# A decoder layer with 32 experts: pooling branch ahead of the state space scans on VectorE, bias-row product and second embedding projection later on TensorE

## The chip, the core and the metric

The kernel runs on one core of a Trainium2 chip. The metric is the device time of one execution in microseconds (us), median of several. The engines named below are PE (TensorE, matrix products), DVE (VectorE), ACT (ScalarE), POOL (GpSimd) and SP (SyncE, which here issues most of the transfers). Each engine works through its own instruction list; semaphores hold an instruction until what it reads is there.

## The reference

One layer over 512 tokens of width 1024, everything in float32. Cut to what the change touches:

```python
proj = h @ w_in                       # 512 x 3072: u_ssm | u_pool | gate_a | gate_b
y_ssm  = s5_branch(u_ssm, ...)        # linear recurrence over the 512 positions
y_pool = pool_branch(u_pool, ...)     # causal means over 2, 4, 8, 16 positions, minus u; group product; projection
merged = sigmoid(gate_a) * y_ssm + sigmoid(gate_b) * y_pool
h = layer_norm(alpha * h + merged @ w_out)
# mixture: top 4 of 32 experts per token, each expert g, u, down with biases
moe_out = sum_k weight_k * (((clip(u) + 1) * g * sigmoid(1.702 g)) @ w_down[e] + b_down[e])
ple = sigmoid(h @ w_ple_gate) * (p @ w_ple_proj)
h = layer_norm(alpha * h + moe_out + ple)
```

## The kernel before

Three stages follow one another. The **front** (to some 377 us) holds the dense work: the input projection, the scans, the pooling branch, the gates, `w_out`, the first layer norm, the routing and the embedding (`ple`) products. The **experts** follow, 32 of them in a fixed order, each with 12 weight tiles of 1 MB (four for gate, four for up, four for down) that SyncE loads into `eraw` tiles. A **tail** adds up and does the second layer norm.

*Products in the front.* A float32 product is made of three: both operands are split into a high and a low part (`split`, L103 to L104: ACT casts the high part, DVE subtracts for the low one), and `mm3` (L115 to L117) adds hi·hi, lo·hi and hi·lo in PSUM. A full product here is 128x128 times 128x512.

*The scans and the pooling.* `chan_major` generators make the projections channel by channel; a loop over 24 slots steps them and calls side work at fixed slots, from tables of four numbers each. `QVEC`, `QTAB`, `QMAT`, `QOUT`, `QST`, `QY` place the steps of the four scan groups: POOL makes tables of powers (`er`, `ei`), DVE makes `hre` and `him`, and `q_y` (L500 to L502) reads them on PE. `PVEC` = (4, 5, 7, 9) places `pool_vec` (L543), which for a window of 2 to 16 adds shifted copies on DVE (`wa`, L551 and L552), scales, and splits the result into `ph` (high part on ACT, low part on DVE); there is one buffer each of `wa` and `ph`. `PMAT` = (4, 6, 7, 9) places `pool_mat`, three products `tp<-ph` on PE, whose result is scaled, split and stored in `mh`, `ml`.

*Routing and the embedding.* `route_vec` picks the experts and ends with `ri` (L812), the list rows; POOL then scatters 16 times into the lists in memory, `lst` (L817). `route_cols` makes `ir`, the rows of the bias tables, takes it through a small product with `one` (L858) and casts it to `ib`. Behind the lists POOL loads them back: `ls` (L993) and, in four pieces, `ls4` (L996); DVE turns `ls4` into `ix4`, the scatter indices of the experts (a `ts` with `jc`, L182, shown in the trace as `ix<-ls,jc`). Overflow beyond the fixed list lengths is counted by a chain of small steps: `cps` and `pcc` (products L1027 and L1030), `bi`, `ov`, a product with `tri` (L1039) into `pps`, then `bx` and the count `nbx`. SyncE reads `nbx` into a register (L1448) ahead of the further `eraw` loads in its list.

The embedding is done in two halves of 512 columns. `ple_g`, and for the second half a loop at L1063 to L1080, make the gating products into `acc` tiles; `ple_p` (L934 to L936) projects `p`; `ple_mul` multiplies the two into `gl`. `base_b` (L945) adds the experts' down-biases to `h`, `base_out` adds `gl` and, for the second half, sends `h` to `acc_d` in memory. In the loop over four bundles of gating products, `base_b` comes with the middle two and `ple_p(1)` before the last.

*What sets the order.* Instructions are put on each engine's list by a scheduler that takes those that are ready by its own reckoning in the order of a priority, which is the order in the code; `tc.high_priority()` puts what it encloses first, `tc.issue_after(x)` puts what it encloses behind instruction x. On the chip each engine keeps the resulting list. Memory of the front that becomes free behind the last gating product is where most of the 16 `eraw` tiles lie: five are loaded at about 208 to 227 us, the others as front tiles are given up. The experts' first biases come through `bias_rows` (four gathers into `br`, by `ib`) and `bias_table` (`btab`).

Of the kernel before, what the change touches and what calls it, by code (L numbers as in the profile page):

```python
# [23 lines left out]
T, D, E, K = 512, 1024, 32, 4  # L24
# [17 lines left out]
EBUF = 2  # L42
ENG = 'SSSVP'
PVEC = (4, 5, 7, 9)
PMAT = (4, 6, 7, 9)
QVEC = (0, 4, 10, 15)
QTAB = (2, 4, 9, 14)
QMAT = (3, 8, 11, 17)
# [20 lines left out]
def _layer(top, tc, nc, x, xT, pT, ssm, ssm_d, log_step, w_in, w_val, w_glg, w_pg, pscale, w_pp,  # L69
           w_out, ln1_g, ln1_b, w_r, b_r, w_gate, b_gate, w_up, b_up, w_down, b_down, w_pleg,  # L70
           w_plep, ln2_g, ln2_b, out, dbg):
    V = nc.vector
# [14 lines left out]
    def tps():  # L87
        return psum.tile([128, 512], F32, tag="tp", name="tp", bufs=2)
# [489 lines left out]
    def at(slot, f, *a):  # L578
        side.setdefault(slot, []).append((f, a))

    for g in range(4):
        at(PVEC[g], lambda g: PV.update({g: pool_vec(g)}), g)
        at(PMAT[g], lambda g: pool_mat(g, PV[g]), g)
    for hs in range(4):
        for f_, sl in ((q_vec, QVEC), (q_tab, QTAB), (q_mat, QMAT), (q_out, QOUT), (q_state, QST), (q_y, QY)):
# [251 lines left out]
    def route_cols():  # L837
        col, cmp_ = RT["col"], RT["cmp"]
        tt(cmp_, col[:, None, :].to_broadcast([128, E, E]), ie[:, :, None].to_broadcast([128, E, E]), OP.is_equal)
        tt(cmp_, cmp_, ie[:, None, :].to_broadcast([128, E, E]), OP.mult)  # L840
        ef = mide.tile([128, 2, E], F32, name="ef")
        V.tensor_reduce(ef[:, 0], cmp_, axis=AX.X, op=OP.add)
        ts(eid, ef[0:1, 0], float(D), OP.mult)
        ts(ef[:, 1], ef[:, 0], float(NB), OP.mult)
        ir = mide.tile([1, E, NB, 2], BF16, name="ir")
        tt(ir, ef[0:1, 1][:, :, None, None].to_broadcast([1, E, NB, 2]), ie[0:1, None, :NB, None].to_broadcast([1, E, NB, 2]), OP.add)
        cf = mide.tile([128, 2, E], F32, name="cf")
        lo, hi = CAP.index(128), CAP.index(64)
        ts(cf[:, 0], col, float(hi), OP.is_lt, 32.0, OP.mult)
        ts(cf[:, 1], col, float(lo + CAP.count(128)), OP.is_lt, 32.0, OP.mult)  # L850
        tt(cf[:, 0], cf[:, 0], cf[:, 1], OP.add)
        ts(cf[:, 1], col, float(lo), OP.is_lt, -32.0, OP.mult)
        stt(cf[:, 0], cf[:, 0], 64.0, cf[:, 1], OP.add, OP.add)
        for i, v in enumerate((col, cf[:, 0])):
            V.tensor_copy(rowb[:, i], v[0:1, None, :].to_broadcast([1, NB, E]))
        pb = tps()
        for h_ in range(2):
            TE.matmul(pb[:, 2 * h_:2 * h_ + 2], lhsT=ir.rearrange("p e j a -> p (e j a)")[:, h_ * 128:(h_ + 1) * 128], rhs=one[0:1, 0:2], start=True, stop=True)  # L858
        V.tensor_copy(ib, pb[:, 0:4].rearrange("p (h a) -> p h a", a=2)[:, :, 0])
# [70 lines left out]
    def ple_p(n0, t_, o):  # L930
        wp = PW["p", n0]
        c_ = slice(t_ * 128, (t_ + 1) * 128)
        for kx in range(2):
            TE.matmul(o, lhsT=pth[:, kx, c_], rhs=wp[0][:, kx], start=kx == 0, stop=False)  # L934
            TE.matmul(o, lhsT=pth[:, kx, c_], rhs=wp[1][:, kx], start=False, stop=False)
            TE.matmul(o, lhsT=ptl[:, kx, c_], rhs=wp[0][:, kx], start=False, stop=kx == 1)  # L936
        PW["o", n0, t_] = o

    def ple_mul(n0, t_):
        tt(PW[n0, t_], PW["o", n0, t_], PW[n0, t_], OP.mult)  # L940
# [79 lines left out]
    with tc.issue_after(RT["ri"].ins):  # L1020
        for r_ in range(NB):
            V.tensor_copy(cn[:, :, r_], mk)
    NC_ = N_CAND
    cps = tps()[:NC_, :2]
    ones2 = one[:, 0:2]
    for t_ in range(4):
        TE.matmul(cps, lhsT=cn[:, t_].rearrange("p r e -> p (r e)"), rhs=ones2, start=t_ == 0, stop=t_ == 3)  # L1027
    pcc = tps()
    for i in range(2):
        TE.matmul(pcc[:NC_, 2 * i:2 * i + 2], lhsT=rowb[:, i].rearrange("p r e -> p (r e)"), rhs=one[0:1, 0:2], start=True, stop=True)  # L1030
    bi = mide.tile([128, 4], F32, name="bi")
    for r_ in range(NB):
        V.memset(bi[r_ * E:(r_ + 1) * E, 0:1], 128.0 * r_)
    tt(bi[:, 0:1], pcc[:NC_, 2:3], bi[:, 0:1], OP.add)
    stt(bi[:, 2:3], bi[:, 0:1], float(E), pcc[:NC_, 0:1], OP.mult, OP.add)
    ov = mide.tile([128, 2], BF16, name="ov")
    V.tensor_scalar(ov[:NC_], cps, bi[:NC_, 0:1], None, op0=OP.is_gt)
    pps = tps()
    TE.matmul(pps[:NC_, 0:2], lhsT=tri[:NC_, :NC_], rhs=ov[:NC_], start=True, stop=True)  # L1039
    TE.matmul(pps[:1, 256:258], lhsT=one[:NC_, 0:1], rhs=ov[:NC_], start=True, stop=True)  # L1040
    V.tensor_scalar(bi[:NC_, 1:2], ov[:NC_, 0:1], -1e6, 1e6, op0=OP.mult, op1=OP.add)
    tt(bi[:NC_, 1:2], pps[:NC_, 0:1], bi[:NC_, 1:2], OP.add)
    bx = late.tile([128, 4], I32, name="bx")
    nbx = late.tile([1, 1], I32, name="nbx")
    V.tensor_copy(bx[:NC_, 0:1], bi[:NC_, 1:2])
    V.tensor_copy(bx[:NC_, 2:3], bi[:NC_, 2:3])
    V.tensor_copy(nbx, pps[:1, 256:257])
    P.iota(bx[:NC_, 1:2], pattern=[[0, 1]], base=E, channel_multiplier=1)

    ple_wp(0)  # L1050
    for t_ in range(4):
        ple_p(0, t_, sacc())
        ple_mul(0, t_)
    with tc.issue_after(RT['ri'].ins):
        ple_w(1)
        ple_wp(1)
# [491 lines left out]
```

## Time and profile before

| what | us |
|---|---|
| median of 3 executions | 1495.27 |
| lowest and highest | 1493.91, 1495.96 |
| profiled execution, its device time | 1496.11 |
| its span in the trace | 1494.4 |
| PE busy in it | 1354.0 |
| DVE busy | 439.3 |
| ACT busy | 245.8 |
| POOL busy | 292.5 |

The profiled execution lies 0.84 us above the median, and 1.71 us of it lie outside the span. The mean granted clock of TensorE in it was 0.975. A row of a timeline reads: start in us, duration in us, engine, line of the kernel, operation, out<-in, shapes, count, and in brackets how long the engine was idle before it and what released it. Starts of neighbouring products lie closer than their durations, since products are pipelined. `tp`, `ss` and `acc` are PSUM tiles.

### The profile page before, as it was taken

Reading aid. Unit: us, or ns where it says so; the run is one execution under the profiler, and the core shown is the slowest. Engines: PE = TensorE matmul, PEld = TensorE weight load, DVE = VectorE, ACT = ScalarE, POOL = GpSimd, SP = SyncE. Lnnn points to the kernel's source line nnn. Section 1 sums busy time; section 2 is a strip of 40 time slices with the busy share of each in tenths; the row PEclk is TensorE's granted clock in tenths of the full one; section 3 lists DMA queues with packets and bytes.
Section 4 is the critical chain, followed back from the end, with each engine's and each line's share of the span. In section 5 each row is a group of like instructions: output and inputs, shape, how many; then the busy total and the mean of one; then the engine's idle time right before and its main releaser. Section 6 shows DMA issues by size and latency. Waiting matters only on the chain.

```text
span 1494.4 us, 41207 instructions
## 1 busy us (share of the span) xinstructions
PE 1354.0 (91%) x18454; PEld 874.6 (59%) x18454; DVE 439.3 (29%) x938; ACT 245.8 (16%) x435; POOL 292.5 (20%) x295
## 2 busy tenths in 40 slices
PE   8969999989799999998897989989889799799993
PEld 7858878767456666665454545545445455456651
DVE  7967657676211111111111101111111111011106
ACT  4534344151101010100000000110000000010011
POOL 0684110016202111111111111112111111110132
PEclk9989999999899999999999999999999999999996
DMA  7213244623999999999999999999999999999953
GB/s 249 85 44 89 59 159 155 217 99 137 351 403 393 397 387 383 396 396 385 386 393 391 391 398 389 397 393 389 387 388 393 383 392 397 378 390 403 404 184 134
DMA packets 105860, 468.58 MB, mean 314 GB/s; under 512 B 17837, under 2 KB 42865, under 8 KB 56528
## 3 DMA queue, kind: packets, MB, share of 16 engines
q1 hardware_dynamic: 88944, 446.12, 76.9%
q0 software_dynamic: 16736, 19.79, 6.1%
q8 instruction: 146, 2.39, 0.6%
q14 instruction: 34, 0.28, 0.1%
HBM read 453.23 MB, written 17.80 MB: 315 GB/s over the span
## 4 chain that ended last, share of the span: by engine, by line
DMA 51%; PE 35%; DVE 7%; POOL 4%; issue 2%; ACT 1%; SPq 0%; POOLq 0%; DVEq 0%; ACTq 0%
DMA eraw<-in_w_down_dram 17%; DMA eraw<-in_w_gate_dram 16%; DMA eraw<-in_w_up_dram 16%; PE acc L1124 13%; PE ss L1124 6%; PE acc L116 3%; PE acc L117 3%; PE acc L115 3%; POOL lst L817 1%; DMA br<-in_b_up_dram,ib 1%; PE acc L1131 1%; DVE h L190 1%; DVE lo L104 1%; PE acc L879 1%; PE tp L1140 1%
## 5 line engine op out<-in xcount | busy, mean ns | idle before, releaser
L1124 PE MATMUL acc<-eraw,xt 128*32 128x256 f32 x10880 | 615.5, 385 | 53.0 <-DMA eraw<-in_w_up_dram 50.0
L1124 PEld LDWEIGHTS acc<-eraw,xt 128*32 128x32 f32 x10880 | 349.1, 111 | 307.0 <-DMA eraw<-in_w_up_dram 68.7
L1124 PE MATMUL ss<-eraw,ht 128*32 128x256 f32 x5312 | 299.7, 380 | 23.0 <-DMA eraw<-in_w_down_dram 22.8
L1159 POOL DMA_INDIRECT acc_d<-y,ix x83 | 129.5, 1560 | 866.5 <-ACT y L1193 850.6
L1124 PEld LDWEIGHTS ss<-eraw,ht 128*32 128x32 f32 x5312 | 170.8, 110 | 148.0 <-DMA eraw<-in_w_down_dram 35.0
L1141 ACT COPY ht<-tp 128x512 f32<-128x512 f32 (+1 forms) x50 | 23.9, 516 | 650.9 <-PE tp L1140 650.9
L182 DVE TENSOR_SCALAR u<-acc 128x512 f32<-128x512 f32 (+1 forms) x51 | 30.6, 600 | 287.5 <-PE acc L1124 276.3
L180 DVE TENSOR_SCALAR g<-acc 128x512 f32<-128x512 f32 (+1 forms) x51 | 30.6, 602 | 275.1 <-PE acc L1124 274.9
L1005 DVE COPY xt<-tp 128x384 f32<-128x384 f32 (+2 forms) x32 | 16.4, 512 | 319.5 <-PE tp L1004 319.5
L1174 ACT ACTIVATE s<-g 128x512 f32<-128x512 f32 (+1 forms) x51 | 27.9, 559 | 270.7 <-DVE g L180 270.7
L104 DVE TENSOR_TENSOR lo<-raw,hi 128x1024 fp32r<-128x1024 f32 (+1 forms) x50 | 60.6, 1216 | 27.9 <-ACT hi L103 27.6
L103 ACT CAST hi<-raw 128x1024 fp32r<-128x1024 f32 (+1 forms) x53 | 54.9, 1036 | 75.4 <-PE acc L116 48.6
L115 PE MATMUL acc<-ahi,hi 128*128 128x512 f32 x160 | 63.9, 399 | 0.0
L117 PE MATMUL acc<-ahi,lo 128*128 128x512 f32 x160 | 63.7, 398 | 0.0
L116 PE MATMUL acc<-alo,hi 128*128 128x512 f32 x160 | 63.4, 396 | 0.0
L1011 POOL DMA_INDIRECT xg<-hd,ls x32 | 32.3, 1011 | 42.4 <-PE tp L1004 28.2
L1207 PE MATMUL acc<-btab,sel_e 128*128 128x512 f32 x102 | 28.3, 387 | 9.6 <-DVE btab L190 9.6
L117 PEld LDWEIGHTS acc<-ahi,lo 128*128 128x128 f32 x160 | 30.6, 191 | 6.6
L115 PEld LDWEIGHTS acc<-ahi,hi 128*128 128x128 f32 x160 | 30.8, 192 | 6.1
L116 PEld LDWEIGHTS acc<-alo,hi 128*128 128x128 f32 x160 | 30.6, 191 | 6.3
L1193 ACT ACTIVATE y<-ss,ls 128x256 f32<-128x256 f32 x83 | 33.8, 481 | 0.0
L186 DVE TENSOR_TENSOR g<-g,s 128x512 f32<-128x512 f32 (+1 forms) x51 | 29.2, 601 | 13.0 <-ACT s L1174 13.0
(404 smaller groups left out, 1303.8 us busy)
## 6 DMA issues: line engine op xcount, KB each, us to landing
eraw<-in_w_gate_dram SPq DMA_DIRECT2D x128, 1024.0 KB, 21.7
eraw<-in_w_up_dram SPq DMA_DIRECT2D x128, 1024.0 KB, 21.5
eraw<-in_w_down_dram SPq DMA_DIRECT2D x128, 1024.0 KB, 23.2
raw<-in_w_in_dram SPq DMA_DIRECT2D x23, 512.0 KB, 4.4
raw<-in_w_out_dram SPq DMA_DIRECT2D x8, 512.0 KB, 4.2
raw<-in_w_ple_gate_dram SPq DMA_DIRECT2D x8, 512.0 KB, 5.5
raw<-in_w_pool_proj_dram SPq DMA_DIRECT2D x4, 512.0 KB, 3.5
raw<-in_w_glu_val_dram SPq DMA_DIRECT2D x4, 512.0 KB, 3.5
```

What stands on the lines that cost most here:

```text
L103: S.copy(h, v)
L104: (lo_eng or V).tensor_tensor(l, v, h.bitcast(F32), op=OP.subtract)
L115: TE.matmul(o, lhsT=lh, rhs=rh, start=start, stop=False)
L116: TE.matmul(o, lhsT=lh, rhs=rl, start=False, stop=False)
L117: TE.matmul(o, lhsT=ll, rhs=rh, start=False, stop=stop)
L180: V.tensor_scalar(o, i, a, None, op0=op)
L182: V.tensor_scalar(o, i, a, b, op0=op, op1=op1)
L186: V.tensor_tensor(o, a, b, op=op)
L1011: P.indirect_dma_start(out=xg[:n_], out_offset=None, in_=hd, in_offset=bass.IndirectOffsetOnAxis(ap=lst_[:n_, 0:1], axis=0), bounds_check= ...
L1124: TE.matmul(os[b // 2][j * 32:(j + 1) * 32, b % 2 * 256:b % 2 * 256 + 256], lhsT=x_, rhs=w_[:, kk, j * 256:(j + 1) * 256], start=first and ...
L1159: q_ = P.indirect_dma_start(out=acc_d.rearrange("t (j c) -> (t j) c", j=4), out_offset=bass.IndirectOffsetOnAxis(ap=ix_[b], axis=0), in_=y ...
L1193: S.activation(y_[:, b * 256:(b + 1) * 256], py[b // 2][:, c_], AF.Copy, scale=w_.bitcast(F32))
```

## The change

Three things are done.

1. The four `pool_vec` calls run under high priority, and the third and fourth `pool_mat` are one slot later.
2. The product with `ir` and its cast become a function of their own, `route_ib`; it and the whole overflow chain are issued behind the first half's `ple_p`.
3. The second half's `ple_p` is issued behind the last gating product.

```diff
-PMAT = (4, 6, 7, 9)
+PMAT = (4, 6, 8, 10)
...
+    def pool_first(g):
+        with tc.high_priority():
+            PV[g] = pool_vec(g)
+
     for g in range(4):
-        at(PVEC[g], lambda g: PV.update({g: pool_vec(g)}), g)
+        at(PVEC[g], pool_first, g)
         at(PMAT[g], lambda g: pool_mat(g, PV[g]), g)
...
-        pb = tps()
+        RT["ir"] = ir
+
+    def route_ib():
+        ir, pb = RT["ir"], tps()
...
-            TE.matmul(o, lhsT=ptl[:, kx, c_], rhs=wp[0][:, kx], start=False, stop=kx == 1)
+            PW["pe"] = TE.matmul(o, lhsT=ptl[:, kx, c_], rhs=wp[0][:, kx], start=False, stop=kx == 1)
...
-    NC_ = N_CAND
-    cps = tps()[:NC_, :2]
...
     ple_wp(0)
     for t_ in range(4):
         ple_p(0, t_, sacc())
         ple_mul(0, t_)
+    with tc.issue_after(PW["pe"].ins):
+        route_ib()
+        NC_ = N_CAND
+        cps = tps()[:NC_, :2]
...
-        if i == order[3]:
-            for t_ in range(4):
-                ple_p(1, t_, (tps if t_ < 2 else sacc)())
...
-                TE.matmul(og[t_], lhsT=hl_, rhs=w2[0][:, k], start=False, stop=sp_)
+                PW["ge"] = TE.matmul(og[t_], lhsT=hl_, rhs=w2[0][:, k], start=False, stop=sp_)
...
+    for t_ in range(4):
+        with tc.issue_after(PW["ge"].ins):
+            ple_p(1, t_, (tps if t_ < 2 else sacc)())
```

The lines left out in the moved block are the same before and after.

**On the engines.** (Line numbers behind L600 are up to 9 higher in the new kernel: L945 is L952 there, L1078 to L1080 are L1084 to L1086, L1037 is L1050, L1039 is L1052.) TensorE's list at the third `pool_mat` (`tp<-ph`), before:

```order
L116 MATMUL acc<-alo,hi 128x512
L117 MATMUL acc<-ahi,lo 128x512
L115 MATMUL tp<-ph,wgh 128x512
L116 MATMUL tp<-ph,wgh 128x512
L117 MATMUL tp<-ph,wgl 128x512
L115 MATMUL acc<-ahi,hi 128x512
L116 MATMUL acc<-alo,hi 128x512
```

and after, where `L500` to `L502` are the first scan group's `q_y`:

```order
L116 MATMUL acc<-alo,hi 128x512
L117 MATMUL acc<-ahi,lo 128x512
L115 MATMUL tp<-ph,wgh 128x512
L116 MATMUL tp<-ph,wgh 128x512
L117 MATMUL tp<-ph,wgl 128x512
L500 MATMUL ss<-t_472,u_t 128x128
L501 MATMUL ss<-qm_473,hre 128x128
L502 MATMUL ss<-qm_474,him 128x128
```

The three products with `ph` have moved behind 24 more `acc` products, and now stand directly ahead of `q_y`.

VectorE's list at the first scan group (`hre`, `him`) and the third `ph`, before:

```order
L483 MEMSET hre 128x4
L484 MEMSET him 128x4
L186 TENSOR_TENSOR hre<-zr,er 128x4x127
L186 TENSOR_TENSOR him<-zr,ei 128x4x127
L286 TENSOR_TENSOR wu_1202<-par,pw 128x320
L186 TENSOR_TENSOR ph<-pu,ph 128x512
L186 TENSOR_TENSOR hre<-hre,zr 128x4x127
L186 TENSOR_TENSOR him<-him,zi 128x4x127
L186 TENSOR_TENSOR ml<-pu,mh 128x512
```

and after:

```order
L483 MEMSET hre 128x4
L484 MEMSET him 128x4
L186 TENSOR_TENSOR hre<-zr,er 128x4x127
L186 TENSOR_TENSOR him<-zr,ei 128x4x127
L186 TENSOR_TENSOR ph<-pu,ph 128x512
L286 TENSOR_TENSOR wu_1202<-par,pw 128x320
L186 TENSOR_TENSOR hre<-hre,zr 128x4x127
L186 TENSOR_TENSOR him<-him,zi 128x4x127
L186 TENSOR_TENSOR ml<-pu,mh 128x512
```

The third `ph` has moved ahead of one row, `wu`.

VectorE's list at `ix` (the tile `ix4`) late in the front, before; `h` are the quarters of the residual, `tp` and `ss` the PSUM tiles with the down-biases, `gl` the embedding:

```order
L186 TENSOR_TENSOR h_2274<-h_2274,gl 128x512
L186 TENSOR_TENSOR h_2273<-h_2273,gl 128x512
L190 SCALAR_TENSOR_TENSOR h_2276<-h_2276,tp 128x512
L190 SCALAR_TENSOR_TENSOR h_2275<-h_2275,tp 128x512
L190 SCALAR_TENSOR_TENSOR h_2274<-h_2274,ss 128x512
L190 SCALAR_TENSOR_TENSOR h_2273<-h_2273,ss 128x512
L182 TENSOR_SCALAR ix_2979<-ls_2974,jc 128x128
L186 TENSOR_TENSOR gl<-tp,gl 128x512
L186 TENSOR_TENSOR h_2276<-h_2276,gl 128x512
L186 TENSOR_TENSOR gl<-tp,gl 128x512
```

and after:

```order
L866 CAST ib<-tp 128x2
L104 TENSOR_TENSOR wp<-raw,wp 128x1024
L186 TENSOR_TENSOR bi<-tp,bi 128x1
L182 TENSOR_SCALAR ix_2979<-ls_2974,jc 128x128
L190 SCALAR_TENSOR_TENSOR bi<-bi,tp 128x1
L1050 TENSOR_SCALAR ov<-tp,bi 128x2
L1059 CAST bx<-bi 128x1
L1054 TENSOR_SCALAR bi<-ov 128x1
L186 TENSOR_TENSOR bi<-tp,bi 128x1
L1060 CAST nbx<-tp 1x1
L1058 CAST bx<-bi 128x1
L190 SCALAR_TENSOR_TENSOR h_2276<-h_2276,tp 128x512
```

The instruction `ix<-ls,jc` stood behind the last `h` row with a down-bias; it now stands between two `bi` rows, ahead of `ov`, `nbx` and all eight `h` rows with a down-bias.

TensorE's list at the overflow product (`tri`), before:

```order
L936 MATMUL ss<-wp,ptl 128x512
L935 MATMUL ss<-wp,pth 128x512
L936 MATMUL ss<-wp,ptl 128x512
L1039 LDWEIGHTS tri
L1039 MATMUL tp<-ov,tri 128x2
L1040 LDWEIGHTS one
L1040 MATMUL tp<-ov,one 1x2
L934 MATMUL ss<-wp,pth 128x512
L935 MATMUL ss<-wp,pth 128x512
```

and after:

```order
L1084 MATMUL acc<-hi,ahi 128x512
L1052 LDWEIGHTS tri
L1052 MATMUL tp<-ov,tri 128x2
L1053 LDWEIGHTS one
L1053 MATMUL tp<-ov,one 1x2
L871 MATMUL tp<-ident,w_2299 96x128 x4
L1085 MATMUL acc<-lo,ahi 128x512
L1086 MATMUL acc<-hi,alo 128x512
L1084 MATMUL acc<-hi,ahi 128x512
L1085 MATMUL acc<-lo,ahi 128x512
L952 MATMUL tp<-bdn,wdt 128x512 x2
```

In both it reads `ov`. Before, `ov` stood 23 rows ahead of `ix` on VectorE; after, it stands behind it. Behind the `tri` product come, after, 50 gating products (L1084 to L1086) and the eight of `base_b` (L952), and then the 24 of `ple_p(1)`.

## Rows read from the trace of the kernel before

**Rows 1.** The chain that ended last, share of the span by engine
```profile
DMA 51%; PE 35%; DVE 7%; POOL 4%; issue 2%; ACT 1%; SPq 0%; POOLq 0%; DVEq 0%; ACTq 0%
```

**Rows 2.** Busy time in one stretch of 5 us; columns in the first line
```profile
core 0: us, PE busy (x) PEld busy (x) DVE busy (x) ACT busy (x) POOL busy (x), PEclk, DMA share, GB/s
...
370.00:375.00 5.00, 5.00 (x24) 4.13 (x23) 1.28 (x3) 0.74 (x2) 1.61 (x2) 1.00 0.16 41
```

**Rows 3.** TensorE's instructions in time at the first scan; start, duration, instruction, idle before
```profile
76.24 0.39 PE L115 MATMUL acc<-ahi,hi 128*128 128x512 f32 x1
...
81.69 0.39 PE L115 MATMUL tp<-ph,wgh 128*128 128x512 f32 x1
93.68 0.80 PE L116 MATMUL tp<-ph,wgh 128*128 128x512 f32 x1 [11.60 <-DVE ph L186]
...
99.39 0.57 PE L117 MATMUL acc<-ahi,lo 128*128 128x512 f32 x1
...
103.00 0.39 PE L502 MATMUL ss<-qm,him 128*128 128x128 f32 x2
```

**Rows 4.** VectorE in time, 41 to 96 us, pooling and the first scan
```profile
41.94 0.69 DVE L552 TENSOR_TENSOR wa<-pu 128x511 f32<-128x511 f32 x1
...
80.94 0.69 DVE L186 TENSOR_TENSOR hre<-ss,ei 128x512 f32<-128x512 f32 x1 [1.40 <-POOL ei L290]
...
91.88 1.74 DVE L186 TENSOR_TENSOR ph<-pu,ph 128x512 fp32r<-128x512 f32 x1
...
95.22 0.71 DVE L186 TENSOR_TENSOR him<-him,zi 128x508 f32<-128x508 f32 x1
```

**Rows 5.** GpSimd in time: start of the tables, one form twice
```profile
48.02 0.49 POOL L329 COPY eb<-sm 128x16 f32<-128x16 f32 x1 [43.98 <-DVE sm L186]
...
67.61 0.80 POOL L285 TENSOR_TENSOR ta<-er 128x64 f32<-128x64 f32 x1
...
80.98 0.29 POOL L285 TENSOR_TENSOR ta<-er 128x64 f32<-128x64 f32 x1
```

**Rows 6.** TensorE in time, at the bias-row product
```profile
344.99 0.20 PE L858 MATMUL tp<-one,ir 1*128 1x2 bf16 x2 [3.07 <-DVE ir L186]
```

**Rows 7.** ScalarE in time, its cast of the second projection's weights
```profile
344.06 1.04 ACT L103 CAST wp<-raw 128x1024 fp32r<-128x1024 f32 x1 [1.96 <-DVE ef L842]
```

**Rows 8.** GpSimd in time: last scatter, loads of the lists, last write of h
```profile
360.15 1.43 POOL L817 DMA_INDIRECT lst<-pay,ri  x1 [0.30 <-issue]
367.09 0.60 POOL L993 DMA_DIRECT2D ls<-lst  x1 [5.51 <-DMA lst<-pay,ri]
367.69 2.24 POOL L996 DMA_DIRECT2D ls<-lst  x4
...
379.92 0.53 POOL L952 DMA_DIRECT2D acc_d<-h  x1 [0.83 <-DVE sel_e L1200]
```

**Rows 9.** DMA issues of 338 to 357 us: count, median us from issue to landing
```profile
lst<-pay,ri POOLq DMA_INDIRECT x13, 2.1
```

**Rows 10.** DMA issues of 340 to 460 us: count, KB each, median us to landing
```profile
eraw<-in_w_gate_dram SPq DMA_DIRECT2D x12, 1024.0 KB, 11.2
```

**Rows 11.** VectorE in time, the scatter indices and the last h
```profile
373.68 0.47 DVE L182 TENSOR_SCALAR ix<-ls,jc 128x128 int32<-128x128 int32 x1 [9.34 <-DMA ls<-lst]
...
378.93 0.69 DVE L186 TENSOR_TENSOR h<-h,gl 128x512 f32<-128x512 f32 x1
```

**Rows 12.** SyncE's queue in time, first weight loads behind the count
```profile
357.84 2.73 SPq L1231 DMA_DIRECT2D eraw<-in_w_up_dram  x3
```

**Rows 13.** SyncE's waits of 330 to 520 us: total, times, longest
```profile
SPq L1231 <- PE acc L1080: 16.4, 1, 16.4
SPq L1448 <- DVE nbx L1047: 15.9, 1, 15.9
```

**Rows 14.** TensorE in time, last gating product and the start of the experts
```profile
377.15 0.39 PE L1080 MATMUL acc<-hi,alo 128*128 128x512 f32 x1
...
400.90 1.01 PE L1207 MATMUL acc<-btab,sel_e 128*128 128x512 f32 x2 [9.57 <-DVE btab L190]
```

More of the change, by code (lines that the diff above doesn't have):

```diff
@@ L1022, in _layer @@
             V.tensor_copy(cn[:, :, r_], mk)
-    NC_ = N_CAND
-    cps = tps()[:NC_, :2]
-    ones2 = one[:, 0:2]
-    for t_ in range(4):
[L1027 to L1048, printed above, removed]
     ple_wp(0)
@@ L1053, in _layer @@
         ple_mul(0, t_)
+    with tc.issue_after(PW["pe"].ins):
+        route_ib()
+        NC_ = N_CAND
+        cps = tps()[:NC_, :2]
+        ones2 = one[:, 0:2]
+        for t_ in range(4):
+            TE.matmul(cps, lhsT=cn[:, t_].rearrange("p r e -> p (r e)"), rhs=ones2, start=t_ == 0, stop=t_ == 3)
+        pcc = tps()
+        for i in range(2):
+            TE.matmul(pcc[:NC_, 2 * i:2 * i + 2], lhsT=rowb[:, i].rearrange("p r e -> p (r e)"), rhs=one[0:1, 0:2], start=True, stop=True)
+        bi = mide.tile([128, 4], F32, name="bi")
+        for r_ in range(NB):
+            V.memset(bi[r_ * E:(r_ + 1) * E, 0:1], 128.0 * r_)
+        tt(bi[:, 0:1], pcc[:NC_, 2:3], bi[:, 0:1], OP.add)
+        stt(bi[:, 2:3], bi[:, 0:1], float(E), pcc[:NC_, 0:1], OP.mult, OP.add)
+        ov = mide.tile([128, 2], BF16, name="ov")
+        V.tensor_scalar(ov[:NC_], cps, bi[:NC_, 0:1], None, op0=OP.is_gt)
+        pps = tps()
+        TE.matmul(pps[:NC_, 0:2], lhsT=tri[:NC_, :NC_], rhs=ov[:NC_], start=True, stop=True)
+        TE.matmul(pps[:1, 256:258], lhsT=one[:NC_, 0:1], rhs=ov[:NC_], start=True, stop=True)
+        V.tensor_scalar(bi[:NC_, 1:2], ov[:NC_, 0:1], -1e6, 1e6, op0=OP.mult, op1=OP.add)
+        tt(bi[:NC_, 1:2], pps[:NC_, 0:1], bi[:NC_, 1:2], OP.add)
+        bx = late.tile([128, 4], I32, name="bx")
+        nbx = late.tile([1, 1], I32, name="nbx")
+        V.tensor_copy(bx[:NC_, 0:1], bi[:NC_, 1:2])
+        V.tensor_copy(bx[:NC_, 2:3], bi[:NC_, 2:3])
+        V.tensor_copy(nbx, pps[:1, 256:257])
+        P.iota(bx[:NC_, 1:2], pattern=[[0, 1]], base=E, channel_multiplier=1)
     with tc.issue_after(RT['ri'].ins):
@@ L1067, in _layer @@
                     base_out(0, t_)
-        if i == order[3]:
-            for t_ in range(4):
-                ple_p(1, t_, (tps if t_ < 2 else sacc)())
         for t_ in range(4):
@@ L1084, in _layer @@
                 PW[1, t_] = gl
+    for t_ in range(4):
+        with tc.issue_after(PW["ge"].ins):
+            ple_p(1, t_, (tps if t_ < 2 else sacc)())
     for t_ in range(4):
```

## The prediction

> **What bounds the kernel now.** I read the chain that ended last first: 51 % of the span is transfers, 35 % TensorE [rows 1]. So there are two places where time can move: the front, where TensorE sets the pace until the weights stream, and the point at which the stream of weights gets going. From there on the stream sets the end, and a delay or gain at its start is carried to the last instruction. Next I read the timelines of all engines around the lines that the diff touches. At the first scan TensorE stands still for 11.60 us, for a `ph` from VectorE [rows 3]. At the bias-row product it stands for 3.07 us [rows 6]. And in the stretch from 370 to 375 us the transfers are at 0.16 of their time though weights are still to come [rows 2]: SyncE first waited 15.9 us for the overflow count `nbx`, and then 16.4 us for a gating product of the embedding (L1080) whose front memory the next weight tile takes [rows 13]. So the front's last gating product, at 377.15 + 0.39 = 377.54 [rows 14], opens the stream. Whatever moves that product moves the end. One row more matters: VectorE waited 9.34 us before `ix` at 373.68, for the landing of the lists [rows 11]. Before, this cost nothing, since no product of TensorE stood behind it.
>
> **Part 1, pooling ahead of the scans.** The order of the new kernel puts 24 full products ahead of the third `pool_mat`. A full product steps by (81.69 − 76.24) / 24 = 0.227 us [rows 3], so 5.45 us of TensorE's 11.60 us can be filled. That is the upper end of the gain only if what stands behind the wait is not later, and `q_y` now stands right behind it. The third `ph` itself is only one row earlier in VectorE's list: it still stands behind `hre`, which waits for GpSimd's tables (80.94) [rows 4]. Priority does not help it, because the scan rows are ready by the scheduler's reckoning before it.
>
> The tables start at 48.02, on VectorE's last `sm` [rows 5]. In the new order six long pooling rows of 0.6 to 0.69 us [rows 4] and some small ones come ahead of that `sm`, in all about 4.3 us. Part of it comes back, since the tables then run beside a VectorE with less to do: the same form took 0.80 us on GpSimd at 67.61, while VectorE was busy, and 0.29 us at 80.98 [rows 5]. I take 2.5 us as given back, an estimate from that pair, and 1.8 us later for the tables; the bounds are 0 and 4.3.
>
> The third `ph` ended at 91.88 + 1.74 = 93.62. It passes one row; I take 0.95 us for it, at the lower side of the rows there (0.7 to 1.7) [rows 4], so 92.65 + 1.8 = 94.45. Behind it come `wu`, `hre`, `him`, and `him`, which ended at 95.22 + 0.71 = 95.93 [rows 4], ends at some 97.7. TensorE reached the row of `q_y` with `him` at 103.00 [rows 3]; now it can be there at 97.7, 5.3 us earlier. From that goes the half clock: after the wait of 11.60 us thirteen products took 99.39 − 93.68 = 5.71 us where they take 13 × 0.227 = 2.95 at the full clock, so 2.76 were lost [rows 3]. That loss stays after the shorter wait, and since `q_y`'s products fall into it I take half of it, 1.4 to 1.5, as not hidden. **Part 1: −3.8 us**, between −5.6 (tables not later) and −1.3 (4.3 later). TensorE is busy nearly throughout from 100 to 340 us, so the gain is carried to the routing.
>
> **Part 2, the bias-row product behind the first projection.** The 3.07 us before L858 end at 344.99 [rows 6]. They are not all gained: TensorE then goes on to the first projection, whose weights ScalarE casts from 344.06 to 345.10 [rows 7]. That is as late as the wait was; I count −0.3 us.
>
> What costs is where VectorE's rows have gone. `ix` now stands ahead of `ov`, `nbx` and the eight `h` rows with a down-bias. `ix` reads the lists; they are loaded back behind the 16 scatters, and these start at a fixed distance from `ri`, which the change does not move. The last scatter is issued at 360.15 and lasts to 361.58; the loads are issued from 367.09, after 5.51 us of idle for its landing, and take 0.60 + 2.24 us to issue, so the last of them is out at 369.93 and `ix` starts 3.75 us later [rows 8, 11]. In that time four weight tiles were on the way (the three at 357.84 and one more before SyncE's wait) [rows 12, 13]. Now they are not, because `nbx` stands behind `ix`. Undisturbed scatters landed in 2.1 us [rows 9], so the last is there at 360.15 + 2.1 = 362.3, the loads are out at 362.3 + 2.84 = 365.1, and `ix` starts between 2.1 and 3.75 us later, from 367.2 to 368.9; I take 368.0. The worst bound is 373.68, nothing quicker than before.
>
> Engines keep their order: the `ix` row shows VectorE idle for 9.34 us with work in its list that needed no list [rows 11]. The Trainium skill, PSUM — Partial Sum Buffer, section Engine vs sequencer instructions, states that "ScalarE/VectorE/GpSimdE queues are strict FIFO", which speaks against this change; the row agrees. By that rule the sum is what follows, without it the first rival below. The Trainium skill, DMA: Bandwidth & Descriptors, section Anatomy of one DMA, gives about 2.0 us plus bytes / 436e3 for a transfer; for the 64 KB of a list load that is an estimate of 2.15 us, with which the final sum would be +4.7 and not +5.4; no row here shows a list load undisturbed.
>
> So TensorE, which reaches the `tri` product at about 358 us, waits for `ov`. That comes 0.75 us behind `ix` (its 0.45 step [rows 11] and two small rows), at 368.75. Behind it stand 50 gating products and 8 of the down-bias: 58 × 0.227 = 13.2 us; small products and transposes add 0.6; a wait this long left the products at half clock before, 2.7 us lost [rows 3]. 368.75 + 16.5 = 385.25, against 377.54: **+7.7 us** for the start of the stream. With the bounds of `ix` it is +6.9 to +13.4. The four tiles held back by `nbx` hide here: SyncE gets the count at about 370, and four tiles issued together are in by some 370 + 11.2 = 381 [rows 10], ahead of 385.25.
>
> Note that +7.7 does not move with part 1: if the front is 3.8 us earlier, `ri`, the scatters and the lists are 3.8 us earlier too. So the two add.
>
> **Part 3, the second projection behind the last gating product.** It takes 24 × 0.227 = 5.45 us out of TensorE's work ahead of that product. This is a real gain for the stream, and is contained in the 385.25 (without it the product would end 5.45 us later still). It is paid at the other end: the last `h` row came at 378.93 + 0.69 = 379.62, 2.08 us behind the last gating product [rows 11, 14]; now the projection lies between, so it ends at 385.25 + 5.45 + 1.4 = 392.1, 12.5 us later, where the weights are 7.7 later. GpSimd gathers the bias rows behind the last write of `h`, at 379.92 [rows 8], so the bias rows come 4.8 us later against the weights. TensorE already waited for their table at 400.90, for 9.57 us [rows 14]. The weights meanwhile fill a ring of 16 tiles; a tile lands 11.2 us after its issue [rows 10], so several are under way at any time, and part of the 4.8 us is absorbed. Bounds 0 and 4.8; I take **+1.5 us**.
>
> **The sum.** −3.8 + 7.7 + 1.5 = +5.4 us (the −0.3 is inside the 7.7). Against the profiled execution, span 1494.4 and device time 1496.11, that is a span of 1499.8 and a time of 1501.5. That execution lay 0.84 us above the median, so the median should be **1500.7 us**.
>
> **Rivals.** *The change does what it says* (faster). If the lists have landed when VectorE comes to `ix`, at some 357 us, nothing is held, and the last gating product ends 5.45 + 0.3 us earlier: −5.75, with part 1 −9.5, a time of 1485.7. For it: the projection's 24 products do leave the path. Against it: the last scatter is only issued at 360.15 [rows 8]. 8 %.
>
> *The landing is not quicker without the weights* (slower still). `ix` stays at 373.68: +13.4, with the bias rows at +3, since less time is left to make up, and −3.8: +12.6, so 1507.9. For it: the list loads spend 2.24 us on issue alone, and the scatters share GpSimd's queue with them. Against it: 2.1 us for the undisturbed scatters [rows 9]. 15 %.
>
> *The two sides cancel* (no change). Part 1 brings its upper end, 5.6, `ix` its lower bound, +6.9, and the bias rows cost nothing: +1.3, 1496.6. 17 %.
>
> **How the numbers follow.** The forecast, between +2 and +9, has 60 %. The range from 1493.5 to 1508.0 takes in the third and second rival and leaves out the first and small tails. A measurement of this kernel tells some 0.2 %, 3 us, from no change: faster by more 9 %, within 20 %, slower by more 71 %.
>
> **What would show it.** On VectorE in the new trace, a wait before `ix` from about 357 to 368 us (less what the front gains), with `ov` behind it; on TensorE a wait of some 10 us before the `tri` product, with products at 0.43 us behind it; SyncE's wait for `nbx` longer by some 12 us, and the transfers idle there. The wait before the third `ph` product should be about 6 to 8 us, and `q_y` some 4 us earlier. The prediction is wrong if `ix` shows no wait, if the front's end is not earlier by 1 to 6 us, or if the first table of the biases comes over 5 us later than the shift of the weights.

## The result, and the profile after

The changed kernel takes 1506.55 us (1504.73 to 1507.91, 4 runs) against 1495.11 of the kernel before: a ratio of 1.0082, 95 % interval 1.0069 to 1.0095, some 11 us slower. The time is inside the range of the prediction, on the side that was forecast, and about twice as far from the kernel before as the forecast's 5.4 us. Its profiled execution took 1504.73 us, with a span of 1503.0: 8.6 us more than the span before. That execution was the fastest of the four, and the one before lay above its median, so the rows below account for 8.6 us; what the other executions have on top, no row shows.

The chain that ended last has hardly changed (before: [rows 1]):

```profile
DMA 50%; PE 35%; DVE 8%; POOL 4%; issue 2%; ACT 1%; SPq 0%; DVEq 0%; POOLq 0%; ACTq 0%
```

The wait that the prediction is about is on VectorE. Its timeline, late in the front (`ix` before: [rows 11]):

```profile
351.32 0.15 DVE L186 TENSOR_TENSOR bi<-tp,bi 128x1 f32<-128x1 f32 x1
365.02 0.33 DVE L182 TENSOR_SCALAR ix<-ls,jc 128x128 int32<-128x128 int32 x1 [13.55 <-DMA ls<-lst]
...
365.33 0.21 DVE L1050 TENSOR_SCALAR ov<-tp,bi 128x2 bf16<-128x2 f32 x1
...
388.34 0.69 DVE L186 TENSOR_TENSOR h<-h,gl 128x512 f32<-128x512 f32 x1
```

`ix` now holds VectorE for 13.55 us, from 351.5 to 365.02, and `ov`, which TensorE needs, stands behind it. TensorE, at the first projection, at the `tri` product, at the last gating product, at the first product with the bias table (before: [rows 6, 14]):

```profile
341.29 0.73 PE L941 MATMUL ss<-wp,pth 128*128 128x512 f32 x2 [3.01 <-ACT wp L103]
...
365.60 0.19 PE L1052 MATMUL tp<-ov,tri 128*128 128x2 bf16 x1 [12.85 <-DVE bx L1059]
...
381.64 0.39 PE L1086 MATMUL acc<-hi,alo 128*128 128x512 f32 x1
...
413.59 1.01 PE L1216 MATMUL acc<-btab,sel_e 128*128 128x512 f32 x2 [12.85 <-DVE btab L190]
```

The 3.07 us before the bias-row product have become 3.01 us before the projection; then TensorE stands 12.85 us at the `tri` product. The row names `bx`, a row of VectorE that ended in the same group; `ov` is what the product reads. The last gating product ends at 381.64 + 0.39 = 382.03, 4.5 us later than before. The first product with the bias table comes at 413.59, 12.7 us later than before, and had been waited for, for 12.85 us.

GpSimd, at its first, its sixth and its last scatter, the loads of the lists, and the last write of `h` (before: [rows 8]):

```profile
335.27 1.37 POOL L821 DMA_INDIRECT lst<-pay,ri  x1 [0.32 <-DVE ri L816]
...
342.53 3.52 POOL L821 DMA_INDIRECT lst<-pay,ri  x1 [0.30 <-issue]
...
357.72 0.96 POOL L821 DMA_INDIRECT lst<-pay,ri  x1 [0.30 <-issue]
360.43 0.60 POOL L1000 DMA_DIRECT2D ls<-lst  x1 [1.75 <-DMA lst<-pay,ri]
361.03 2.24 POOL L1003 DMA_DIRECT2D ls<-lst  x4
...
389.33 0.53 POOL L959 DMA_DIRECT2D acc_d<-h  x1 [0.83 <-DVE sel_e L1209]
```

The lists are indeed faster without weights beside them: the wait for the last scatter's landing fell from 5.51 to 1.75 us. SyncE's issues of weights, and its wait for the count (before: [rows 12, 13]):

```profile
367.50 1.52 SPq L1240 DMA_DIRECT2D eraw<-in_w_up_dram  x3
369.07 14.26 SPq L1240 DMA_DIRECT2D eraw<-in_w_gate_dram  x4
383.38 2.12 SPq L1240 DMA_DIRECT2D eraw<-in_w_up_dram  x4
393.03 8.10 SPq L1238 DMA_DIRECT2D eraw<-in_w_down_dram  x4
419.39 5.51 SPq L1240 DMA_DIRECT2D eraw<-in_w_gate_dram  x3
```

```profile
SPq L1457 <- DVE bx L1058: 33.7, 1, 33.7
```

The first four tiles start 9.7 us later, held by the count; those behind the last gating product 4.4 us later. The hole behind the `down` tiles, which lay between 383.62 + 10.92 = 394.54 and 407.21 before, has grown from 12.7 to 18.3 us, from 393.03 + 8.10 = 401.13 to 419.39: the ring of 16 tiles is full, since TensorE stands at the bias table. Before:

```profile
383.62 10.92 SPq L1229 DMA_DIRECT2D eraw<-in_w_down_dram  x4
407.21 8.10 SPq L1231 DMA_DIRECT2D eraw<-in_w_gate_dram  x4
```

In the changed kernel the transfers run dry shortly after. The same stretch of 10 us in both kernels, and one long stretch that takes in the whole start of the stream, first of the kernel before and then of the changed one (columns as in [rows 2]):

```profile
430.00:440.00 10.00, 10.00 (x192) 5.98 (x184) 1.85 (x4) 1.01 (x2) 0.00 (x0) 1.00 1.01 414
350.00:500.00 150.00, 137.41 (x1977) 87.74 (x1979) 36.75 (x67) 15.66 (x30) 35.71 (x36) 0.97 0.92 351
```

```profile
430.00:440.00 10.00, 10.00 (x170) 6.40 (x174) 0.56 (x2) 1.18 (x3) 0.94 (x1) 1.00 0.68 247
350.00:500.00 150.00, 121.77 (x1731) 77.95 (x1733) 30.96 (x62) 13.57 (x28) 33.28 (x34) 0.91 0.86 323
```

In 430 to 440 us the transfers fell from 1.01 to 0.68 of their time. In 350 to 500 us the kernel before moved 351 GB/s x 150 us = 52.7 MB, the changed one 323 x 150 = 48.5 MB. At the 2.62 us per MB that the next section finds over all kernels, the missing 4.2 MB would cost 11.0 us; the span grew by 8.6, since the kernel before lies 1.7 us above the line found there, and the changed one 0.7 below it.

### The profile page after: what moved, and what is told of

The parts are those of the page before. It is cut to its first block, busy times and chain, and to the rows that moved or that the text cites. A ratio compares the mean times of both kernels' runs of the same rounds, so it can differ in the third digit from the quotient of the medians.

```text
span 1503.0 us, 41207 instructions
## 1 busy us (share of the span) xinstructions
PE 1353.8 (90%) x18454; PEld 874.9 (58%) x18454; DVE 440.7 (29%) x938; ACT 246.4 (16%) x435; POOL 292.9 (19%) x295
## 4 chain that ended last, share of the span: by engine, by line
DMA 50%; PE 35%; DVE 8%; POOL 4%; issue 2%; ACT 1%; SPq 0%; DVEq 0%; POOLq 0%; ACTq 0%
DMA eraw<-in_w_down_dram 20%; DMA eraw<-in_w_up_dram 15%; PE acc L1133 13%; DMA eraw<-in_w_gate_dram 12%; PE ss L1133 7%; PE acc L116 3%; PE acc L117 3%; PE acc L115 3%; POOL lst L821 1%; DMA br<-in_b_up_dram,ib 1%; PE acc L1140 1%; DVE lo L104 1%; PE tp L1149 1%; DVE h L190 1%; PE acc L1216 1%
## 5 line engine op out<-in xcount | busy, mean ns | idle before, releaser
L1012 DVE COPY xt<-tp 128x384 f32<-128x384 f32 (+2 forms) x32 | 16.4, 512 | 315.2 <-PE tp L1011 315.2
L1216 PE MATMUL acc<-btab,sel_e 128*128 128x512 f32 x102 | 28.3, 388 | 12.9 <-DVE btab L190 12.9
```

What stands on the lines that cost most here:

```text
L1216: TE.matmul(os[i][:, :256 * n_], lhsT=SL[c], rhs=btab[:, m_, c // 16, None, :].to_broadcast([128, n_, 256]), start=start, stop=stop, skip_ ...
```

## The experiments

Two causes were to be told apart: the hold of VectorE at `ix` (part 2), and the bias table that comes late against the weights (part 3), besides the gain of part 1. Twelve kernels were run; each ratio is to the kernel before, on the same chip.

**e1: the changed kernel with `ix` late.**

```diff
-        ts(ix4, ls4[:, :, :, 0], float(NB), OP.mult, jc, OP.add)
...
                 if i == 0 and s == 2:
+                    ts(ix4, ls4[:, :, :, 0], float(NB), OP.mult, jc, OP.add)
                     bias_table(br)
```

> The changed kernel with one edit: the instruction that makes the scatter indices (ix, from the lists) is issued with the first bias table instead of ahead of the first expert, so that VectorE does not stand at it. Theory (the hold of VectorE at ix is what the change costs): TensorE's wait of 12.8 us before the tri product is gone, the last gating product ends at about 377.5 - 3.9 - 5.75 = 368 us, the last h row about 4.8 us earlier than in the kernel before; 1485.5 (bias rows cost nothing) to 1490.5 (the end follows the bias table), I say 1488. Rival (the hold is no more than a symptom, the later bias rows or the moved projection cost the time by themselves): still 1503 or more.

Measured: 1500.89 us, ratio 1.0045 (1.0031 to 1.006). By the ratios the hold is worth some 5.5 us here, and more than half of the loss is left. Neither side's figure came. On TensorE:

```profile
363.45 1.22 PE L952 MATMUL tp<-bdn,wdt 96*128 96x512 f32 x2 [5.09 <-ACT wdt L872]
...
409.99 1.01 PE L1216 MATMUL acc<-btab,sel_e 128*128 128x512 f32 x2 [9.62 <-DVE btab L190]
```

The wait at `tri` is gone, but 5.09 us went into a wait for `wdt`, and the bias table still comes at 409.99, 9.1 us later than before.

**e2: part 1 alone.** The edit is the first two pieces of the diff (`PMAT` and `pool_first`).

> The kernel before with part 1 alone: pooling under high priority, third and fourth pool_mat one slot later. Theory: the wait before the third ph product falls from 11.6 to about 7 us, ri and everything behind it comes 3.9 us earlier, and this reaches the end: 1491.2 (1490 to 1493). Rival (the gain is swallowed on the way, at the lists or the bias rows): 1495, within 0.2 % of the kernel before.

Measured: 1492.94 us, ratio 0.9992 (0.9983 to 1.0002). Not told from no change, though the interval lies mostly on the side of a gain: the rival, within 0.2 %, fits it, and the theory's 3.9 us (a ratio of 0.9974) was not reached.

**e3: the changed kernel with early bias gathers.** The gathers get a tile of their own and are written behind the overflow chain, ahead of the second half's weights; GpSimd has them ahead of the writes of `h`.

```diff
+    br = late.tile([128, D], F32, name="br").rearrange("p (h m c) -> p h m c", h=2, m=2)
+    for h_ in range(2):
+        for m_, b_ in enumerate((b_gate, b_up)):
+            P.indirect_dma_start(out=br[:, h_, m_], ...)
     with tc.issue_after(RT['ri'].ins):
         ple_w(1)
...
-        br = bias_rows()
```

> The changed kernel with one edit: the four gathers of bias rows have a tile of their own and are issued on GpSimd ahead of the writes of h instead of behind them. VectorE still stands at ix. Theory (the stream opens 4.5 us late, and what is on top of that, some 7 us, comes from the bias table that is late against the stream): the wait for the table, 12.9 us in the changed kernel, falls below 3 us, and the time falls to 1495.1 + 4.5 = 1499.6 or below (1496 to 1501). Rival (the stream's late opening alone costs all 11.4, its delay grows by slower transfers): 1506 as in the changed kernel.

Measured: 1499.73 us, ratio 1.0036 (1.0022 to 1.0051). As the theory had it, the wait for the table is gone altogether; what is left, 5.4 us by the ratio, is near the 4.5 of the late opening. On TensorE, the row has no wait:

```profile
402.01 0.61 PE L1224 MATMUL acc<-btab,sel_e 128*128 128x512 f32 x2
```

**e4: part 3 alone.** The edit is the last three pieces of the diff: `ple_p(1)` behind the last gating product.

> The kernel before with part 3 alone: the second half's projection behind the last gating product. The last gating product ends 5.45 us earlier (372.1), the last h row and so the bias table stay where they were. Theory one (the opening of the stream and the bias table each count, the later of the two against the ring): 1490 to 1494, a gain of 1 to 5. Theory two (the bias table alone sets the end at this place): 1495, no change. Theory three (the opening alone): 1489.7.

Measured: 1499.86 us, ratio 1.0036 (1.0023 to 1.0048): slower, which none of the three theories had. SyncE, TensorE, the stretch behind, and the landing of the first gathers (the last view's columns as in [rows 10]):

```profile
374.26 2.09 SPq L1231 DMA_DIRECT2D eraw<-in_w_up_dram  x4
392.81 8.10 SPq L1229 DMA_DIRECT2D eraw<-in_w_down_dram  x4
```

```profile
382.87 1.51 PE L1004 MATMUL tp<-ident,xg 96*128 96x96 f32 x8 [4.48 <-DMA xg<-hd,ls]
...
409.22 1.00 PE L1207 MATMUL acc<-btab,sel_e 128*128 128x512 f32 x2 [8.72 <-DVE btab L190]
```

```profile
420.00:430.00 10.00, 8.44 (x124) 5.25 (x120) 2.70 (x6) 1.30 (x3) 0.94 (x1) 1.00 0.71 275
```

```profile
br<-in_b_gate_dram,ib POOLq DMA_INDIRECT x2, 20.9
```

The weights do start 4.7 us earlier (374.26 against 378.93), so more of them lie ahead of the small transfers that GpSimd issues. The tokens of the first expert are waited for, 4.48 us; the bias gathers land in 20.9 us, against 13.9 in the kernel before, and the table comes 8.3 us later than before. Then the ring is full and the transfers fall to 0.71, where the kernel before has 1.02 in the same stretch. The projection was moved out of the stream's way, and the stream then ran over what it needs.

From the profiles so far I made a sum with two limits, the opening of the stream and the bias table, which the next four were to try.

**e5: the changed kernel with `ix` late and early bias gathers** (the edits of e1 and e3).

> The changed kernel with both edits: ix late, and the bias gathers ahead of the writes of h. From the profiles so far a sum with two limits fits: span = the later of (SyncE's first weight load behind the last gating product + 1114) and (the first product with the bias table + 1089). With ix late the first was 379.6, so a span of 1493.7 and 1495 us (1493 to 1497), if the 5.1 us that TensorE waited for wdt come again; without that wait 1490. Rival (what is left over is not the bias table): 1501 as with ix late alone.

Measured: 1494.96 us, ratio 1.0002 (0.9993 to 1.0012). With both undone the loss is gone. The 5.09 us of e1 did not come again; instead TensorE waited 6.53 and 7.09 us for the tokens of the first two experts. So the figure came, but not by the way of the sum. And since two waits of e1 went at once, `wdt` and the table, e5 does not say what each was worth; the table's part rests on e3.

```profile
381.92 1.51 PE L1011 MATMUL tp<-ident,xg 96*128 96x96 f32 x8 [6.53 <-DMA xg<-hd,ls]
```

**e6: part 3 with early bias gathers.**

> The kernel before with part 3 and the early bias gathers. Theory of two limits: the stream opens at 374.3 as with part 3 alone, the table no longer limits: a span of 1488.3, 1490 us (1488 to 1492). Rival (an earlier stream is itself what hurts, since it pushes back the gathers of tokens and other small transfers): 1497 to 1500 as with part 3 alone.

Measured: 1491.84 us, ratio 0.9983 (0.9974 to 0.9991). Part 3 turns from a loss of 5.4 into a gain of 2.5 us when the bias gathers don't stand behind the writes of `h`. The rival fell.

**e7: the kernel before with early bias gathers.**

> The kernel before with the early bias gathers alone. Theory of two limits: the opening of the stream (378.9 + 1114) is the later limit before, the table (400.9 + 1089) the earlier by 3 us, so no change: 1494 (1492 to 1496), though TensorE's wait of 9.6 us for the table is gone. Rival (the 9.6 us count): 1485 to 1490.

Measured: 1493.44 us, ratio 0.9995 (0.9986 to 1.0005). TensorE's 9.57 us at the table [rows 14] were worth nothing that can be told in the kernel before: its transfers stayed at 1.01 to 1.02 of their time from 390 to 450 us. Of e6's gain of 2.5 us, some 0.7 may be the early gathers' own, by this run.

**e8: part 2 alone.** `route_ib` and the moved overflow chain, without `PMAT`, `pool_first` and the moved `ple_p(1)`.

> The kernel before with part 2 alone: bias-row product and overflow chain behind the first projection. VectorE stands at ix as in the changed kernel, and the second projection lies ahead of the last gating product again. Theory of two limits: the last gating product at about 390.7, the stream opens at 392, span 1506, 1507.6 us (1504 to 1510), with the bias table not the limit. Rival (part 3 is what cost in the changed kernel, part 2 alone is harmless): 1494 to 1497.

Measured: 1506.7 us, ratio 1.0088 (1.0074 to 1.0102). Part 2 alone costs all that the whole change costs. TensorE and SyncE:

```profile
368.41 0.18 PE L1048 MATMUL tp<-ov,tri 128*128 128x2 bf16 x1 [11.37 <-DVE bx L1055]
...
411.95 1.01 PE L1212 MATMUL acc<-btab,sel_e 128*128 128x512 f32 x2 [4.11 <-DVE btab L190]
```

```profile
391.22 2.71 SPq L1236 DMA_DIRECT2D eraw<-in_w_up_dram  x4
```

The `tri` product waits 11.37 us, the stream opens 12.3 us later than before; the table is waited for only 4.11 us.

**e9: parts 1 and 3 with early bias gathers, no part 2.**

> The kernel before with parts 1 and 3 and the early bias gathers, without part 2. Part 1 brought ri 2.2 us earlier on the mean of the profiles so far (335.3, 338.2, 336.9, 336.2, 338.3 with it; 339.1, 338.6, 339.4, 337.7, 338.1 without: about 1.6 to 2.2), part 3 with early bias rows measured 1491.8. Theory (the two add): 1489.8 (1488.5 to 1491.5), faster than the kernel before by about 0.3 %. Rival (part 1's gain is swallowed by the token gathers, which wait for the lists): 1491.8.

Measured: 1487.72 us, ratio 0.9962 (0.995 to 0.9974). Faster than both kernels, by the ratios 5.7 us below the one before and 18 below the changed one. The time lies 0.8 us below the range expected, and the ratio, a gain of 0.38 %, near the expected 0.3: the kernel before, too, took only 1493.01 us beside it. The rival, that part 1's gain is swallowed, fell.

**e10: the same, with the first weights held behind the lists.**

```diff
-    V.tensor_copy(nbx, pps[:1, 256:257])
+    nb0 = late.tile([1, 1], I32, name="nb0")
+    V.tensor_copy(nb0, pps[:1, 256:257])
...
+    with tc.issue_after(RT["ls"].ins):
+        P.tensor_copy(nbx, nb0)
```

Here `RT["ls"]` is the last load of the lists; the gathers stand behind it too.

> The same with one more edit: the overflow count goes through GpSimd, behind the loads of the lists in its queue, and the bias gathers behind it, so that the first four weight tiles wait until the lists have been asked for; no engine but SyncE waits for it. Theory (small transfers that run beside the weights land late; without the weights they land soon): the scatters land within 2 us of the last issue and not 5.5, TensorE's wait for the first tokens, 6.6 us with part 3 and early bias rows, falls below 2 us. For the time: the four tiles are loaded from about 364.5 to 375 and the stream goes on from there, 375 + 1114 = 1489 of span, 1490 us, as without the hold. Rival (TensorE's start of the experts is the limit, the stream has slack): 1484 to 1487.

Measured: 1495.02 us, ratio 1.0011 (1.0002 to 1.0019): 7 us worse than e9. GpSimd at the loads of the lists, then the long stretch, of e10 and of e9:

```profile
361.74 0.60 POOL L997 DMA_DIRECT2D ls<-lst  x1 [1.78 <-DMA lst<-pay,ri]
```

```profile
350.00:500.00 150.00, 142.00 (x2081) 90.89 (x2083) 35.43 (x66) 15.70 (x30) 35.35 (x35) 0.97 0.92 350
```

```profile
350.00:500.00 150.00, 139.66 (x2082) 88.91 (x2084) 34.05 (x61) 15.09 (x29) 33.68 (x33) 0.97 0.98 373
```

The scatters landed 1.78 us after the last issue, as expected. But TensorE's wait for the first tokens fell to 4.45 us only, as the bias gathers had gone ahead of them on GpSimd. And the time did not stay: the stream's first tiles started 12.9 us later than in e9 (366.11 against 353.20), and this was not made up. In the long stretch it is 350 against 373 GB/s, or 52.5 against 56.0 MB. I had counted on the idle time behind those four tiles to take them up; there was none to spare: in e9 the transfers are at 0.91 of their time from 360 to 370 us already, and behind part 3 the opening comes at 368.82.

**e11: all three parts, `ix` late, early gathers, count behind the lists.**

> The changed kernel (all three parts) with ix late, the early bias gathers, and the count through GpSimd behind the lists. Theory: as the one before, the last gating product some us earlier does not help, since the four tiles wait for the lists: 1489 to 1492. Rival (what is left is the front): 1484 to 1487.

Measured: 1497.94 us, ratio 1.0032 (1.0021 to 1.0044), above both figures. This fits e10's reason: the count stood behind three gathers, and the first tiles started at 371.7.

**e12: the later slots without the priority,** with part 3 and early gathers.

> The kernel before with the later pool_mat slots of part 1 but without its high priority, with part 3 and the early bias gathers. In the changed kernel GpSimd's tables start 3.6 us later (51.6 against 48.0) and end 2.1 us later, since pooling rows stand ahead of the last sm. Theory (the slots bring all of part 1's gain, the priority takes 2 us of it back): the tables start at 48 again, TensorE's wait before the third ph is about 6 us, the first q_y with him comes at about 96 (98.1 in the changed kernel), and the time is 2 us below the version with all of part 1 (1487.7): 1485.7 (1484 to 1487.5). Rival (the priority helps, by pooling of the other groups): 1488 to 1492.

Measured: 1487.35 us, ratio 0.9967 (0.9955 to 0.9979), the same as e9. GpSimd's tables and TensorE at the third `ph`:

```profile
47.76 0.49 POOL L329 COPY eb<-sm 128x16 f32<-128x16 f32 x1 [43.73 <-DVE sm L186]
```

```profile
93.45 0.79 PE L116 MATMUL tp<-ph,wgh 128*128 128x512 f32 x1 [6.03 <-DVE ph L186]
...
95.76 0.80 PE L502 MATMUL ss<-qm,him 128*128 128x128 f32 x2
```

The tables start at 47.76 again (51.61 in the changed kernel), and the first `q_y` with `him` comes at 95.76. In the rows at the scan the slots do all of part 1's work and the priority takes 2 us back; at the first scatter 0.5 us of that is left (334.02 against 334.56 in e9), and in the time it is not to be seen. So the theory is half shown.

**What all of them have in common.** The bytes moved in 350 to 500 us (rate x 150 us) against the span of the same profiled execution, one of each kernel:

| kernel | GB/s, 350 to 500 us | MB | span us |
|---|---|---|---|
| changed | 323 | 48.5 | 1503.0 |
| e8 | 323 | 48.5 | 1504.6 |
| e1 | 334 | 50.1 | 1498.5 |
| e4 | 339 | 50.9 | 1497.3 |
| e3 | 341 | 51.2 | 1497.9 |
| e11 | 342 | 51.3 | 1496.0 |
| e10 | 350 | 52.5 | 1492.6 |
| before | 351 | 52.7 | 1494.4 |
| e5 | 353 | 53.0 | 1490.9 |
| e7 | 353 | 53.0 | 1491.4 |
| e6 | 356 | 53.4 | 1491.5 |
| e2 | 360 | 54.0 | 1489.3 |
| e12 | 372 | 55.8 | 1484.3 |
| e9 | 373 | 56.0 | 1484.0 |

A straight line through them, span = 1630.6 − 2.62 us per MB, holds all 14 to within 1.7 us; 2.62 us per MB is 382 GB/s, near the 391 GB/s that the kernel before moves from 500 to 1300 us. From 500 to 1300 us every one of the 14 moves 391 or 392 GB/s. So each MB that is not in by 500 us is paid in full at the end, whatever kept it out: a late opening (e8), a dry ring (e4), or tiles held back (e10).

## Why the prediction was right, and where it was off

*The front, −3.8.* The changed kernel's `ri` released the first scatter at 335.27, against 339.14 before: −3.87.

```profile
339.14 1.37 POOL L817 DMA_INDIRECT lst<-pay,ri  x1 [0.32 <-DVE ri L812]
```

But this agreement is partly luck. Over the profiles with all of part 1 (eight) the first scatter comes at 336.5 on the mean (334.6 to 338.3), over those without it (five) at 338.6 (337.7 to 339.4): −2.1. The changed kernel's rows at the scan, of TensorE and of GpSimd:

```profile
94.36 0.80 PE L116 MATMUL tp<-ph,wgh 128*128 128x512 f32 x1 [6.89 <-DVE ph L186]
...
97.51 0.80 PE L501 MATMUL ss<-qm,hre 128*128 128x128 f32 x2 [1.50 <-DVE hre L186]
...
101.24 0.39 PE L500 MATMUL ss<-t,u_t 128*128 128x128 f32 x2
```

```profile
51.61 1.17 POOL L329 COPY eb<-sm 128x16 f32<-128x16 f32 x1 [47.58 <-DVE sm L186]
```

The wait for `ph` fell to 6.89 us (6 to 8 was said), the tables start 3.6 us later (0 to 4.3 was said). Two terms of my sum are off: a second wait, 1.50 us for `hre`, is not in it, and of the half clock I took half as lost. After the shorter wait the granted clock was 0.50 (1.2 GHz) up to some 101.2 and 1.00 (2.4 GHz) behind it; before, the products were slow up to 99.8 [rows 3].

*The hold at `ix`, +7.7.* Right in kind and size: from the `tri` product to the end of the last gating product it is 382.03 − 365.60 = 16.4 us, where I had 16.5. With the front 3.9 us earlier, `ix` was to come at 364.1 and came at 365.02; the last gating product was to end at 381.4 and ended at 382.03. The loads of the lists landed sooner than I took: the last was out at 361.03 + 2.24 = 363.27, and `ix` came 1.75 us behind it, where I took 2.9 from bounds of 2.1 and 3.75. This is below both bounds. The estimate of 2.15 us from the Trainium skill, DMA: Bandwidth & Descriptors, section Anatomy of one DMA, was nearer; the five loads landed 2.1 us after their issue (median):

```profile
ls<-lst POOLq DMA_DIRECT2D x5, 64.0 KB, 2.1
```

What made up for it is the scatters. Their sixth issue took 3.52 us, so the last was issued 2.4 us earlier than before and not 3.9; and from its issue to the first load it was 360.43 − 357.72 = 2.7 us, where I took 2.1. For the order of VectorE's list I had cited [rows 11], and that row can't carry it: the first row behind `ix` there, a product with `gl`, read what ScalarE gave out at 374.10 only, with `ix` already running, so nothing was ready that could have passed it. The changed kernel's row can: a `bi` row and `ov` stood behind `ix` for 13.55 us, and the products that they read had ended by 350.51 + 0.20 = 350.71.

```profile
350.51 0.20 PE L1043 MATMUL tp<-one,rowb 1*128 1x2 bf16 x2
```

This agrees with the section Engine vs sequencer instructions of PSUM — Partial Sum Buffer in the Trainium skill. The four tiles held back by the count did hide, as said: the last of them was issued at 369.07 and landed 12.9 us later, at 382.0, when the last gating product ended.

*The bias rows, +1.5.* This is the step that was mis-sized. The table was to be 8.7 us late against before (12.5 − 3.8); it was 12.7, since the gathers landed in 17.4 us and not in 13.9. The weights behind the last gating product came 4.4 us late, so the table was 12.7 − 4.4 = 8.3 us late against them, over the 5 that the prediction had named as a sign of being wrong: on this step it was wrong by its own test, though the time fell into the range. The DMA issues of the changed kernel in 340 to 460 us (columns as in [rows 10]):

```profile
acc_d<-h POOLq DMA_DIRECT2D x4, 512.0 KB, 13.2
...
br<-in_b_up_dram,ib POOLq DMA_INDIRECT x2, 17.4
tab<-bx POOLq DMA_INDIRECT x1, 17.2
```

I had taken their landing as fixed, though the rows gave 2.1 us for small scatters with nothing beside them [rows 9] and 11.2 for a weight tile [rows 10]. And I took the ring to absorb most of the lateness. If the late opening cost its 4.4 us in full, the table cost 8.6 − 4.4 = 4.2 us in the profiled execution, near the upper bound of 4.8; e3, which takes it away, is 6.9 us below the changed kernel by the ratios, above that bound.

*Part 3, counted as a gain of 5.45 us for the stream.* In the changed kernel parts 1 and 3 together bought nothing: without them e8 is as slow as with them. The stream opened 7.8 us earlier than in e8 (383.38 against 391.22), but the wait at the table was 12.85 us against 4.11. Alone it costs 5.4 us (e4), and only with the gathers moved is it a gain (e6). I had both sides of it in the sum, and the trade came out worse than I weighed it.

*The rivals.* That the change does what it says fell with the hold: without it (e1) the change still lost, and without the late table too (e5) it came out even. No run with part 2 came near its 1485.7. The rival without quicker landing was 1507.9; the time is near it, but the landing was quicker, and the mechanism was another.

*What stays open.* In e1 ScalarE's cast to `wdt` started 5.4 us after the transposes that it reads had ended, and TensorE waited 5.09 us for it; in e5, whose lists on TensorE and ScalarE are the same, it came 6.5 us earlier. ScalarE in e1 and then in e5:

```profile
362.81 0.58 ACT L872 CAST wdt<-tp 96x512 fp32r<-96x512 f32 x1 [8.51 <-remote]
```

```profile
356.33 0.58 ACT L872 CAST wdt<-tp 96x512 fp32r<-96x512 f32 x1 [3.14 <-PE tp L1053]
```

No row tells why, so how much of e1's loss is this wait and how much the table stays open. And the executions of the changed kernel without a profile lie some 2 us above the profiled one.

## What to carry to other kernels

When a stage is bound by a stream of transfers, count the bytes that are in by the time it runs full: here every missing MB cost 2.6 us at the end. Ahead of such a stage look for instructions that wait for a transfer and stand in an engine's list in front of others that don't; an order that reads well in the code can put one there. And before the stream is opened earlier, issue the small gathers that its consumer needs, or, as in e4, the stream makes them late and then stops for them.

## What the runs showed of the hardware that I had not expected

Small gathers land the later, the more lies ahead of them. The four gathers of bias rows, of the same size each time, landed in 3.3 us (median) with no weights ahead of them (e11), in 6.3 with four tiles under way (e9), and in 13.9 before, 17.4 in the changed kernel and 20.9 in e4, where the `up` tiles behind the last gating product had started 1.8, 6.8 and 7.2 us ahead of the first of them. These last three differ from the first two in a second thing: there the gathers also stand behind the four writes of `h`, 512 KB each, in GpSimd's queue, which in the changed kernel took 13.2 us themselves. What the weights add and what these writes add was not tried apart. `tab`, a small transfer on the same queue, landed in 10.2 us in e9, ahead of the writes with the stream open, and in 17.2 us in the changed kernel, behind them, which speaks for both.
